# A two-layer hybrid trunk on one core: head 1's third attention group as a block product, transposes and scores behind other products

## The chip, the cores and the metric

The kernel runs on one core of a Trainium2 chip. The metric is the device time of one execution in microseconds (us), the median of several runs. A profiled execution is a run of its own with a hardware trace; its "span" is the part of it in which the trace sees instructions. Engines: PE (TensorE, the matrix unit; PEld is its weight load), DVE (VectorE), ACT (ScalarE), POOL (GpSimd) and SP (SyncE, which here only issues transfers). Each engine executes its own instructions strictly in the order in which the program holds them.

## The reference

The kernel computes two decoder layers for 512 tokens of width 1024 in float32. Layer 0 is the part that matters here, a dilated attention with 8 heads and 3 groups per head; layer 1 has a pooling mixer in its place, and a SwiGLU feed-forward network follows each.

```
qkv = (h @ w_qkv).reshape(B, S, 3, 3, HEADS, 128)        # 3 groups x (q, k, v) x 8 heads of 128
for g, (window, dil) in enumerate(((128, 1), (512, 4), (2048, 16))):
    o, lse = dilated_window_attention(q_g, k_g, v_g, window, dil, slopes[g])
...
wts = softmax(lse over the 3 groups)
o = sum over groups of wts * o
x = x + o.reshape(B, S, 1024) @ w_out
x = x + (silu(gate) * up) @ w_down                        # behind each mixer
```

So each head needs three q/k pairs (group 0, 1 and 2), the scores of group 0 and of groups 1 and 2, a softmax that is merged over the groups, and values for all three.

## The kernel before

**Products.** A float32 product is made of three matmuls on a high and a low part (hi x hi, hi x lo, lo x hi). The weights come from memory into a ring `raw` of 4 buffers, and ACT (L91, the high part) and DVE (L92, the low part) split them into a ring `w` of 5 buffers. A *plain* product (class `Product`, L325, L326, L328) turns 1024 inputs into 128 columns of q or k for 512 tokens: 24 matmuls of 128 x 512. A *block product* (`seven`, with `mult`, L457 to L459) makes q and k of a group together by Strassen's scheme, in seven products of 12 matmuls of 128 x 256 each; it costs 84 matmuls of half the width in place of 48 of the full one. For it DVE adds up inputs (tiles `T`, made by `prepare`, whose L574, L578, L579 and L583 are DVE work), DVE puts the results together (L498, L504 or L506, L511, L512; ACT copies the first, L485), and the weights need sums too (class `Pair`): SP issues the transfers `b` (L169), `a` (L170) and the half-size `c` (L171), POOL issues a transfer L172 that adds a further piece of memory into `b` once `b` has landed, and DVE adds L188 and L189. A pair is split in four steps, `blocks`, `sums`, `more`, `last`; the split of `sums` needs the accumulated `b`.

**Stages.** Head 0 and, up to `NSOLO`, the groups of head 1 use plain products; all other groups use `seven`. The values of group 0 of an even head and the odd head after it come from one more `seven` (results `vt`); the values of groups 1 and 2 come, after the odd head, from `values12` (L628 to L630; seven products of 24 matmuls of 128 x 256, with a pair of pairs as weights).

**What lies between the products.** After each of the seven products of `seven`, a *hook* (number 0 to 6) may emit other work of the attention. `between(h, g)` (L933) says what, for group `g` of head `h`:
- `scores0` (L712 on PE, 88 small matmuls; DVE L715, L718; ACT L721): scores of group 0.
- `scores12` (L732 and L736 on PE; DVE L739, L742; ACT L746): scores of groups 1 and 2; L732 needs q and k of group 1, L736 those of group 2.
- `scatter` (L753, DVE) and `merge` (L765 on PE; DVE L767 to L779; ACT L782): the merged softmax of a head.
- `turn0` (L795, 4 transposes on PE; ACT L799, L801; DVE L802) and `turn12` (L816, 4 transposes on PE; ACT L817; DVE L821): the probabilities are transposed.
- `turn_values` (L685, 8 transposes on PE; ACT copies): the values of group 0 are transposed, once for two heads.
- `output` (L833 to L843; 30 matmuls on PE): probabilities times values.

**What sets the order.** The program text sets it on PE. On the other engines a scheduler fixes it when the program is built; at run time each engine follows this list. Weights are requested (`pump`) between products, a load as soon as its `raw` buffers are free, a split as soon as its `w` buffer is.

Of the kernel before, what the change touches and what calls it, by code (L numbers as in the profile page):

```python
# [38 lines left out]
K2 = KC // 2  # L39
NPLAIN = 4  # L40
WARM = 5
NSOLO = 3
PARTS = ((0, 2, False), (2, 10, True), (10, 18, True), (18, 22, False))
ENDS = 5
BACK = {"blocks": 3, "sums": 7}
# [19 lines left out]
def trunk(ctx: ExitStack, tc: tile.TileContext, xT, xN, norms, w_first, w_qk, w_qkp, w_v0, w_v0p, w_v12, w_out, w_pair, w_down, w_dblock, w_pin, w_pgrp,  # L65
# [7 lines left out]
    def x_tile(k, name="x", dtype=F32):  # L73
        return cpool.tile([P, S], dtype, tag=f"x{k}", name=name)
# [7 lines left out]
    def ps():  # L82
        return psum.tile([P, S], F32, tag="ps", name="ps")
# [119 lines left out]
    def pump(n=1, must=False):  # L203

        turn[0] += not must
        for i in range(n):
            while loads and all(free(r, c) for r, c in loads[0][1].items()):
                loads[0][0].issued = turn[0]
                loads.popleft()[2]()
            if not steps or not free(steps[0][1]):  # L210
                assert not must
                return
            unit, back = steps[0][0], BACK.get(steps[0][2].__name__)
            if not must and back and unit.back and turn[0] < unit.issued + back:
                return
            steps.popleft()[2]()

    def pairs(*srcs, shift=LINE // 4, back=False):

        these = [Pair(src, shift, back) for src in srcs]  # L220
        for parts in zip(*(p.steps() for p in these)):
            steps.extend(parts)
        units.append((these,))
# [11 lines left out]
    def plain(*srcs, lean=False):  # L235
        for src in srcs:
            share(1, src, lean=lean)

    for h in range(HEADS):
        if h == 0:  # L240
            plain(*[w_qk[u] for u in range(len(QK) - NF)])
        for g in range(3):
            if h == 1 and g < NSOLO:
                plain(*[w_qk[len(QK) - NF + 2 * g + c] for c in range(2)])
            elif h:
                pairs(w_qkp[3 * h - 3 - NSOLO + g])
        if h == 0:
# [123 lines left out]
    def product(layer):  # L371
        return Product(KC, stream(layer)).add(range(KC)).p
# [77 lines left out]
    def in_place(t, a=slice(0, 2)):  # L450
        return t[:, a.start * H2:a.stop * H2]

    def mult(dst, w, half, T, name, n=K2, on=False):
        for k in range(n):
            c = slice(half * w.n + k * P, half * w.n + (k + 1) * P)
            th, tl = T[name, k]
            nc.tensor.matmul(dst, w.t[0][:, c], th, start=k == 0 and not on, stop=False, skip_group_check=on)  # L457
            nc.tensor.matmul(dst, w.t[0][:, c], tl, start=False, stop=False, skip_group_check=on)  # L458
            nc.tensor.matmul(dst, w.t[1][:, c], th, start=False, stop=k == n - 1, skip_group_check=on)  # L459

    def part(unit, name):
        while name not in unit.w:
            pump(must=True)
        return unit.w[name]

    def seven(T, one, two, scratch, after={}, blocks=False):


        (unit,), = units.popleft()
        into, left, right = by_block if blocks else in_place, slice(0, 1), slice(1, 2)  # L470

        def again(v):
            return v.unsqueeze(1).to_broadcast([P, 2, H2])

        p1, p26, p45, p73 = ps(), ps(), ps(), ps()

        def behind(i):
            pump()
            for f in after.get(i, ()):
                f()  # L480

        w = part(unit, "b")
        mult(p1[:, :H2], w, 0, T, "11")
        first, sums = scratch("first"), scratch("sums")
        nc.scalar.copy(first[:, :H2], p1[:, :H2])  # L485
        behind(0)
        mult(p26[:, :H2], w, 1, T, "21")
        w.done()
        behind(1)
        w = part(unit, "s")  # L490
        mult(p45[:, H2:], w, 0, T, "1")
        behind(2)
        mult(p73[:, :H2], w, 1, T, "3")
        w.done()
        behind(3)
        w = part(unit, "m")
        mult(p26[:, H2:], w, 0, T, "2")
        nc.vector.tensor_add(into(one), p26, again(first[:, :H2]))  # L498
        behind(4)
        mult(p73[:, H2:], w, 1, T, "22")  # L500
        w.done()
        if blocks:
            for a in (left, right):
                nc.vector.tensor_add(in_place(sums, a), in_place(p73, a), into(one, right))  # L504
        else:
            nc.vector.tensor_add(sums, p73, again(one[:, H2:]))  # L506
        behind(5)
        w = part(unit, "l")
        mult(p45[:, :H2], w, 0, T, "4")
        w.done()  # L510
        nc.vector.tensor_sub(into(two), p45, again(sums[:, :H2]))  # L511
        nc.vector.tensor_sub(into(one, right), sums[:, H2:], p45[:, H2:])  # L512
        behind(6)
# [82 lines left out]
    with tc.tile_pool(name="opool", bufs=1) as opool:  # L596
        early = opool.tile([P, HEADS, S], F32R, tag="o", name="early")
        with tc.tile_pool(name="apool", bufs=1) as apool:
# [9 lines left out]
            def evac(h, u, p):  # L608
                g, c = QK[u]
                t = apool.tile([P, S], F32, name=f"qk{g}{c}")  # L610
                scaled_by(t, p, g == 0)
                QKV[h, g, c] = t
# [64 lines left out]
            VT = []  # L677
# [174 lines left out]
            H, T, o = {}, {}, []  # L852
# [34 lines left out]
            def scratch(name):  # L887
                return apool.tile([P, S], F32, tag="scratch", name=name, bufs=3)
# [41 lines left out]
            def later(f, *a):  # L930
                return lambda: f(*a)

            def between(h, g):  # L933

                if g == 0:
                    if h % 2:
                        return {1: [later(merge, h - 1)]} if h == 1 else {}
                    return {1: [later(output, h - 2)], 2: [later(merge, h - 1)]}
                if g == (2 if h == 1 else 1):
                    turns = [later(turn0, h - 1), later(turn12, h - 1)]  # L940
                    if h % 2 and h > 1:
                        turns.append(later(turn_values, h - 1))
                    return {1: turns, 3: [later(scores0, h)]}
                return {}

            prepare(0)
            for u in range(NF):
# [17 lines left out]
            for h in range(1, HEADS):  # L965
                for g in range(3):
                    if h == 1 and g < NSOLO:
                        for c in range(2):
                            evac(h, 2 * g + c, product(0))
                        for fs in between(h, g).values():  # L970
                            for f in fs:
                                f()
                    else:
                        for c in range(2):
                            QKV[h, g, c] = apool.tile([P, S], F32, name=f"qk{g}{c}")
                        seven(T, QKV[h, g, 0], QKV[h, g, 1], scratch, between(h, g), g == 0)
                if h == 1:
                    whole = opool.tile([P, HEADS, S], F32, tag="o", name="o")
                    o.extend(whole[:, h, :] for h in range(HEADS))
                if h == HEADS - 1:  # L980
                    X[:] = [x_tile(k) for k in range(KC)]
                    for k in range(KC):
                        nc.gpsimd.dma_start(X[k], xN[:, k, :])
                if h % 2 == 0:
                    VT[:] = [apool.tile([P, S], F32, tag=tag, name="vt") for tag in ("row", "o0")]
                    seven(T, *VT, scratch, {0: [later(scores12, h)], 4: [later(scatter, h), later(output, h - 1)],
                                            5: [later(merge, h)]}, True)
                elif h < HEADS - 1:
                    QKV[h // 2, 12, 2] = values12({0: [later(scores12, h)], 4: [later(scatter, h)]})
                else:  # L990
                    QKV[h // 2, 12, 2] = values12({0: [later(scores12, h)], 1: [later(halve, 0), later(halve, 1)],
                                                   2: [later(scatter, h), later(halve, 2), later(halve, 3)],
                                                   3: [later(merge, h)],
                                                   4: [later(give, ("t", k, 0)) for k in range(2)]
                                                   + [later(halve, 4), later(halve, 5)]})
# [480 lines left out]
```

## Time and profile before

| | before |
|---|---|
| median of 3 runs | 1190.72 us (1189.71 to 1190.86) |
| the profiled execution | 1190.77 us |
| its span | 1187.8 us |
| granted TensorE clock, mean | 0.998 |
| attention of heads 1 to 7 in the span | from about 60 to 415 us |

The span is 3.0 us shorter than the profiled execution's own time. A row of the timeline view reads: start in us, duration in us, engine, line of the program, operation, output and input, shape, how many; in square brackets the idle time before it and the instruction that ended it. Matmuls are pipelined, so their durations overlap: the time that one costs is the distance between two starts. A row of the windows view reads: the stretch, its length, PE's busy time and the number of matmuls that touch the stretch, the granted clock, DMA's share and GB/s.

### The profile page before, as it was taken

The page shows a single profiled execution, that of the slowest core. Times are in us where ns is not written, and L with a number is a line of the kernel's source. Part 1 is how long each engine was busy: PE and PEld are TensorE (multiplying, and loading weights), DVE is VectorE, ACT ScalarE, POOL GpSimd, SP SyncE. Part 2 cuts the span into 40 slices and gives each one's busy share as a digit, 9 for nine tenths or more (in the row PEclk, how much of TensorE's full clock was granted, in tenths as well). Part 3 has the DMA queues.
Part 4 walks back from the last instruction along what each step waited for, and adds up shares of the span by engine and source line. Part 5 has one row for each costly group of instructions (what it writes and reads, how often), then busy time and mean ns, then how long its engine had stood idle before and what let it go on. Part 6 is the DMA issues. An engine that isn't in the chain of part 4 may idle for free.

```text
span 1187.8 us, 24866 instructions
## 1 busy us (share of the span) xinstructions
PE 1180.1 (99%) x9934; PEld 1119.3 (94%) x9934; DVE 965.5 (81%) x1693; ACT 711.1 (60%) x1243; POOL 168.8 (14%) x170
## 2 busy tenths in 40 slices
PE   9999999999999999999999999999999999999997
PEld 7889999999999988889999999988888999999997
DVE  7978988889797855699988997656879998898875
ACT  6545555455455546647756775675575775676553
POOL 1111211111111002311111111122130111111100
PEclk9999999999999999999999999999999999999999
DMA  8346666665766449857777777798695777777732
GB/s 293 116 104 163 156 155 158 169 162 147 193 158 155 143 142 212 184 118 188 198 193 191 195 184 199 202 265 210 125 198 107 191 193 198 200 193 191 198 93 71
DMA packets 82003, 205.18 MB, mean 173 GB/s; under 512 B 7760, under 2 KB 13024, under 8 KB 81888
## 3 DMA queue, kind: packets, MB, share of 16 engines
q1 hardware_dynamic: 51088, 141.96, 36.5%
q0 software_dynamic: 30512, 61.36, 31.2%
q8 instruction: 77, 1.26, 0.4%
q14 instruction: 38, 0.31, 0.1%
q10 hardware_dynamic: 288, 0.29, 0.1%
HBM read 201.48 MB, written 2.10 MB: 171 GB/s over the span
## 4 chain that ended last, share of the span: by engine, by line
PE 98%; issue 1%; ACT 0%; DVE 0%; POOL 0%; DVEq 0%; POOLq 0%
PE ps L457 20%; PE ps L459 19%; PE ps L458 19%; PE ps L325 9%; PE ps L328 8%; PE ps L326 8%; PE ps L628 2%; PE ps L629 2%; PE ps L630 2%; PE ps L918 2%; PE ps L840 1%; PE ps L712 1%; PE ps L732 1%; PE ps L834 1%; PE ps L833 0%
## 5 line engine op out<-in xcount | busy, mean ns | idle before, releaser
L91 ACT ACTIVATE w<-raw 128x1024 fp32r<-128x1024 f32 x265 | 280.6, 1063 | 175.5 <-PE ps L459 76.3
L92 DVE TENSOR_TENSOR w<-raw,w 128x1024 fp32r<-128x1024 f32 x265 | 322.8, 1221 | 58.6 <-ACT w L91 54.8
L457 PE MATMUL ps<-far,w 128*128 128x256 f32 x896 | 246.6, 275 | 0.3 <-ACT first L531 0.3
L458 PE MATMUL ps<-far,w 128*128 128x256 f32 x896 | 246.5, 275 | 0.0
L459 PE MATMUL ps<-far,w 128*128 128x256 f32 x896 | 246.4, 275 | 0.0
L457 PE MATMUL ps<-near,w 128*128 128x256 f32 x640 | 179.3, 280 | 0.0
L458 PE MATMUL ps<-near,w 128*128 128x256 f32 x640 | 177.1, 277 | 0.0
L459 PE MATMUL ps<-near,w 128*128 128x256 f32 x640 | 177.1, 277 | 0.0
L457 PEld LDWEIGHTS ps<-far,w 128*128 128x128 f32 x896 | 168.2, 188 | 0.5 <-ACT first L531 0.5
L458 PEld LDWEIGHTS ps<-far,w 128*128 128x128 f32 x896 | 168.2, 188 | 0.1
L459 PEld LDWEIGHTS ps<-far,w 128*128 128x128 f32 x896 | 168.2, 188 | 0.0
L325 PE MATMUL ps<-near,w 128*128 128x512 f32 (+1 forms) x332 | 125.6, 379 | 0.0
L328 PE MATMUL ps<-near,w 128*128 128x512 f32 (+1 forms) x332 | 124.9, 376 | 0.0
L326 PE MATMUL ps<-near,w 128*128 128x512 f32 (+1 forms) x332 | 124.9, 376 | 0.0
L457 PEld LDWEIGHTS ps<-near,w 128*128 128x128 f32 x640 | 120.5, 188 | 0.4
L458 PEld LDWEIGHTS ps<-near,w 128*128 128x128 f32 x640 | 120.3, 188 | 0.0
L459 PEld LDWEIGHTS ps<-near,w 128*128 128x128 f32 x640 | 120.3, 188 | 0.0
L172 POOL DMA_DIRECT2D raw<-w_pair x36 | 43.6, 1210 | 293.3 <-DMA raw<-w_pair 112.2
L325 PEld LDWEIGHTS ps<-near,w 128*128 128x128 f32 x332 | 62.3, 188 | 11.6 <-ACT near L91 0.4
L326 PEld LDWEIGHTS ps<-near,w 128*128 128x128 f32 x332 | 62.4, 188 | 11.3 <-DVE near L92 0.2
L328 PEld LDWEIGHTS ps<-near,w 128*128 128x128 f32 x332 | 62.3, 188 | 11.4
L91 ACT ACTIVATE half<-rawhalf 128x512 fp32r<-128x512 f32 x81 | 51.0, 630 | 14.7 <-PE ps L459 12.6
(310 smaller groups left out, 2758.2 us busy)
## 6 DMA issues: line engine op xcount, KB each, us to landing
raw<-w_pair SPq DMA_DIRECT2D x80, 512.0 KB, 5.0
raw<-w_qkp SPq DMA_DIRECT2D x36, 512.0 KB, 4.2
raw<-w_pair POOLq DMA_DIRECT2D x36, 512.0 KB, 7.4
raw<-w_dblock SPq DMA_DIRECT2D x32, 512.0 KB, 4.6
raw<-w_v SPq DMA_DIRECT2D x18, 512.0 KB, 4.6
raw<-w_qkp POOLq DMA_DIRECT2D x18, 512.0 KB, 7.6
rawhalf<-w_pair SPq DMA_DIRECT2D x36, 256.0 KB, 5.2
raw<-w_dblock POOLq DMA_DIRECT2D x16, 512.0 KB, 7.4
```

Source lines behind the costliest of these rows:

```text
L91: nc.scalar.activation(hi, v, AF.Copy)
L92: nc.vector.tensor_tensor(lo, v, hi.bitcast(F32), op=OP.subtract)
L172: nc.gpsimd.dma_start(self.b.rearrange("p (a c) -> p a c", a=2), self.src[:, None, 3 * n:].to_broadcast([P, 2, n]), accum_op=OP.add)
L325: nc.tensor.matmul(self.p[:, cols], w[0][:, s], mh[:, cols], start=self.done == 0, stop=False)
L326: nc.tensor.matmul(self.p[:, cols], w[0][:, s], ml[:, cols], start=False, stop=False)
L328: nc.tensor.matmul(self.p[:, cols], w[1][:, s], mh[:, cols], start=False, stop=self.done == self.n)
L457: nc.tensor.matmul(dst, w.t[0][:, c], th, start=k == 0 and not on, stop=False, skip_group_check=on)
L458: nc.tensor.matmul(dst, w.t[0][:, c], tl, start=False, stop=False, skip_group_check=on)
L459: nc.tensor.matmul(dst, w.t[1][:, c], th, start=False, stop=k == n - 1, skip_group_check=on)
L628: nc.tensor.matmul(o, mh, wh, start=k == 0, stop=False)
L629: nc.tensor.matmul(o, mh, wl, start=False, stop=False)
L630: nc.tensor.matmul(o, ml, wh, start=False, stop=k == K2 - 1)
```

## The change

`NSOLO` goes from 3 to 2, so that head 1's group 2 runs through `seven` (with a pair as weights) in place of two plain products. And `between` and the values' hooks place the attention's other work anew:

```diff
-NSOLO = 3
+NSOLO = 2
...
                 if g == 0:
-                    if h % 2:
-                        return {1: [later(merge, h - 1)]} if h == 1 else {}
-                    return {1: [later(output, h - 2)], 2: [later(merge, h - 1)]}
-                if g == (2 if h == 1 else 1):
-                    turns = [later(turn0, h - 1), later(turn12, h - 1)]
-                    if h % 2 and h > 1:
-                        turns.append(later(turn_values, h - 1))
-                    return {1: turns, 3: [later(scores0, h)]}
-                return {}
+                    return {1: [later(merge, h - 1)], 3: [later(turn_values, h - 1)] if h > 1 else []} if h % 2 else {
+                        1: [later(output, h - 2)], 2: [later(merge, h - 1)]}
+                if h == 1 and g:
+                    return {3: [later(turn0, 0)], 5: [later(turn12, 0)], 6: [later(scores0, 1)]} if g == 2 else {}
+                if g == 1:
+                    return {0: [later(turn0, h - 1)], 2 + h % 2: [later(turn12, h - 1)], 4: [later(scores0, h)]}
+                return {} if h % 2 else {2: [later(output, h - 1)]}
...
                 if h % 2 == 0:
                     VT[:] = [apool.tile([P, S], F32, tag=tag, name="vt") for tag in ("row", "o0")]
-                    seven(T, *VT, scratch, {0: [later(scores12, h)], 4: [later(scatter, h), later(output, h - 1)],
-                                            5: [later(merge, h)]}, True)
+                    seven(T, *VT, scratch, {3: [later(scores12, h)], 6: [later(scatter, h)]}, True)
```

So in head 1 `turn0` stands behind the fourth product of group 2, `turn12` behind the sixth and `scores0` behind the seventh. In heads 2 to 7 `turn0`, `turn12` and, in odd heads, `turn_values` no longer stand together but at three places; `scores0` stands one product later; the merge of an even head moves from the values' product into group 0 of the next head; `output` of an odd head moves from the values' product to group 2; and `scores12` of heads 2, 4 and 6 goes from the values' first product to the fourth. Lines behind L933 shift by two or three.

The change moves instructions also on the engines that the text does not order. First DVE's list while head 1's group 0 is computed, at the third input sum of `prepare` (L578 and what follows). Before:

```order
L743 TENSOR_SCALAR nm<-st 128x4
L606 TENSOR_TENSOR qk_698<-ps,row 128x16x16x2
L753 TENSOR_TENSOR far<-st,place 128x64
L92 TENSOR_TENSOR w<-raw,w 128x1024
L578 TENSOR_TENSOR raw<-raw 128x2x256
L579 TENSOR_TENSOR raw<-raw 128x256
L583 TENSOR_TENSOR raw<-raw 128x256
L574 SCALAR_TENSOR_TENSOR raw<-x,nrm,row 128x512
```

and now:

```order
L92 TENSOR_TENSOR near<-raw,near 128x512 x2
L606 TENSOR_TENSOR qk_729<-ps,row 128x16x16x2
L767 TENSOR_TENSOR far<-ps,place 128x64
L770 TENSOR_REDUCE st<-far 128x16
L92 TENSOR_TENSOR w<-raw,w 128x1024
L771 TENSOR_TENSOR mx<-st 128x8
L578 TENSOR_TENSOR raw<-raw 128x2x256
L772 TENSOR_TENSOR ex<-st,mx 128x16
L579 TENSOR_TENSOR raw<-raw 128x256
L774 TENSOR_TENSOR dd<-ex,st 128x16
L583 TENSOR_TENSOR raw<-raw 128x256
L775 TENSOR_TENSOR mx<-dd 128x8
```

Ahead of the first L578 there now stand the second result of group 0 (`qk_729`, the k product), the start of head 0's merge and one split `w` more, the one that needs the `w` buffer which that k product gives back.

Then DVE's list at the end of head 1's group 2 (`s_493`, `s_617` before and `s_496`, `s_620` now are head 0's probabilities; `qk_841`, `qk_873` before and `qk_821`, `qk_822` now are q and k of head 1's group 2). Before:

```order
L92 TENSOR_TENSOR w<-raw,w 128x1024 x2
L188 TENSOR_TENSOR raw<-raw 128x512
L189 TENSOR_TENSOR raw<-raw 128x512
L606 TENSOR_TENSOR qk_841<-ps,row 128x512
L92 TENSOR_TENSOR w<-raw,w 128x1024
L812 MEMSET t_893 128x512
L606 TENSOR_TENSOR qk_873<-ps,row 128x512
L791 MEMSET t_875 128x896
L92 TENSOR_TENSOR w<-raw,w 128x1024
L802 STREAM_TRANSPOSE t_875<-s_493 32x4x32 x4
L821 STREAM_TRANSPOSE t_893<-s_617 32x4x32 x4
```

and now:

```order
L188 TENSOR_TENSOR raw<-raw 128x512
L802 STREAM_TRANSPOSE t_884<-s_496 32x4x32 x4
L92 TENSOR_TENSOR w<-raw,w 128x1024 x3
L498 TENSOR_TENSOR qk_821<-ps,first 128x512
L189 TENSOR_TENSOR raw<-raw 128x512
L506 TENSOR_TENSOR sums<-ps,qk_821 128x512
L812 MEMSET t_933 128x512
L188 TENSOR_TENSOR raw<-raw 128x512
L92 TENSOR_TENSOR w<-raw,w 128x1024
L821 STREAM_TRANSPOSE t_933<-s_620 32x4x32 x4
L511 TENSOR_TENSOR qk_822<-ps,sums 128x512
L512 TENSOR_TENSOR qk_821<-sums,ps 128x256
```

Before, q and k of group 2 are finished by one L606 each. Now they are finished by L511 and L512, which stand last in this list, behind three splits in a row (L92 x3; the third of them is the `sums` step of the second pair of `values12`), a fourth split and the eight small transposes.

Last, DVE's list at the end of head 2's values (`vt`), from the second score of groups 1 and 2 (L739) on. Before:

```order
L739 SCALAR_TENSOR_TENSOR s_1747<-ps,b_1505 128x4x128
L739 SCALAR_TENSOR_TENSOR s_1747<-ps,b_1505 128x4x32
L92 TENSOR_TENSOR half<-rawhalf,half 128x512
L742 TENSOR_REDUCE st<-s_1747 128x4
L743 TENSOR_SCALAR nm<-st 128x4
L92 TENSOR_TENSOR w<-raw,w 128x1024
L753 TENSOR_TENSOR far<-st,place 128x64
L92 TENSOR_TENSOR w<-raw,w 128x1024
L498 TENSOR_TENSOR vt<-ps,first 128x16x16x2
```

and now:

```order
L742 TENSOR_REDUCE st<-s_1874 128x4
L504 TENSOR_TENSOR sums<-ps,vt 128x256
L743 TENSOR_SCALAR nm<-st 128x4
L504 TENSOR_TENSOR sums<-ps,vt 128x256
L188 TENSOR_TENSOR raw<-raw 128x512
L92 TENSOR_TENSOR w<-raw,w 128x1024
L511 TENSOR_TENSOR vt<-ps,sums 128x16x16x2
L512 TENSOR_TENSOR vt<-sums,ps 128x8x16x2
L753 TENSOR_TENSOR far<-st,place 128x64
L189 TENSOR_TENSOR raw<-raw 128x512
L767 TENSOR_TENSOR far<-ps,place 128x64
```

L753, which the matmul L765 of the merge needs, stood ahead of the values' sums; now it stands behind L511 and L512, which end the values.

## The prediction, made before the changed kernel was run

> **What bounds the kernel now.** I read the busy shares first, then the chain of waits, then PE's own waits.
>
> ```profile
> PE   1180.1 (99%) x9934; PEld 1119.3 (94%) x9934; DVE 965.5 (81%) x1693; ACT 711.1 (60%) x1243; POOL 168.8 (14%) x170
> PE 98%; issue 1%; ACT 0%; DVE 0%; POOL 0%; DVEq 0%; POOLq 0%
> PE ps L898 <- DVE idle L895: 1.2, 1, 1.2
> PE ps L457 <- ACT first L531: 0.3, 1, 0.3
> ```
>
> PE is busy for 99% of the span and the chain that ended last is PE for 98%. In the whole trace PE waits twice, 1.5 us together, neither time in the attention. So the time is PE's list. The change can save only what it takes off that list or off the pace at which it is worked through, and it can lose by any wait that it puts there. No wait exists that it could remove.
>
> **Pace.** One 128x256 matmul does not always cost the same. These windows lie between two interruptions each, in heads 1 to 3; the first is plain products, the others hold, by the code, 12, 24, 132, 48, 120, 24 and 120 block matmuls.
>
> ```profile
> 65.69:87.55 21.86, 21.86 (x99) 1.00 0.44 114
> 116.60:118.10 1.50, 1.50 (x15) 1.00 0.72 247
> 127.30:130.30 3.00, 3.00 (x27) 1.00 0.60 175
> 131.60:146.69 15.09, 15.09 (x141) 1.00 0.72 183
> 148.06:153.82 5.76, 5.76 (x58) 1.00 0.66 187
> 158.70:172.41 13.71, 13.71 (x124) 1.00 0.58 133
> 174.07:177.08 3.01, 3.01 (x28) 1.00 0.65 202
> 178.37:192.62 14.25, 14.25 (x129) 1.00 0.47 106
> ```
>
> ```profile
> 126.39 0.28 PE L459 MATMUL ps<-h,w 128*128 128x256 f32 x1
> 126.51 0.60 PE L795 MATMUL ps<-ident,s 128*128 128x128 f32 x4
> 126.94 0.60 PE L816 MATMUL ps<-ident,s 128*128 128x128 f32 x4
> 127.30 0.36 PE L457 MATMUL ps<-near,w 128*128 128x256 f32 x1
> 127.50 0.28 PE L458 MATMUL ps<-near,w 128*128 128x256 f32 x1
> 127.62 0.28 PE L459 MATMUL ps<-near,w 128*128 128x256 f32 x1
> 131.60 0.39 PE L457 MATMUL ps<-near,w 128*128 128x256 f32 x1
> 131.82 0.28 PE L458 MATMUL ps<-near,w 128*128 128x256 f32 x1
> ```
>
> Behind an interruption the first step takes 0.20 to 0.22 us (127.30 to 127.50, 131.60 to 131.82), some 0.09 more than the steps after it. Those then run at one of two paces until the next interruption: (15.09 - 0.22) / 131 = 113.5 ns in the window from 131.60 and (14.25 - 0.22) / 119 = 117.9 ns in the one from 178.37, at a granted clock of 1.00 in both. The price of the slow pace is 4.4 ns per matmul. By the same arithmetic the stretch from 148.06 (behind `scores12` in the values of an even head) is slow, (5.76 - 0.22) / 47 = 117.9, and the one from 158.70 (behind a merge) fast, (13.71 - 0.22) / 119 = 113.4; the short ones from 116.60 (behind `output` in group 0) and 127.30 and 174.07 (behind the transposes) are slow, with a second long step at their end. Behind `scores0` the even head is fast (131.60) and the odd one slow (178.37). Heads 4 to 7 repeat this.
>
> **The change, part by part.** First the product. The first window is groups 1 and 2 of head 1, four plain products, 96 matmuls: group 2 costs half, 10.93 us. In its place come 84 block matmuls, 9.5 us at the fast pace and 9.9 at the slow one. I take 9.7: **-1.2 us**. `turn0`, `turn12` and `scores0` of head 1 stood together and now interrupt three times: 2 x 0.09 = **+0.2**.
>
> Second, head 1's wait. PE's list around it was:
>
> ```profile
> 87.55 0.60 PE L795 MATMUL ps<-ident,s 128*128 128x128 f32 x4
> 89.81 0.39 PE L628 MATMUL ps<-w,near 128*128 128x256 f32 x1
> 92.67 1.05 PE L732 MATMUL ps<-qk,qk 128*128 128x128 f32 x8
> 93.66 0.46 PE L736 MATMUL ps<-qk,qk 128*32 128x32 f32 x32
> ```
>
> With group 2 1.0 us shorter, PE comes to L736 at 93.66 - 1.0 = 92.7. L736 needs L511 and L512, now last in DVE's list, behind three splits of which the third needs the accumulated `b` of the second values pair. How late that is follows from these rows of DVE, ACT, SP and POOL:
>
> ```profile
> 65.87 1.04 ACT L91 ACTIVATE w<-raw 128x1024 fp32r<-128x1024 f32 x1
> 62.90 0.69 DVE L578 TENSOR_TENSOR raw<-raw 128x512 f32<-128x512 f32 x1
> 69.22 1.22 DVE L92 TENSOR_TENSOR w<-raw,w 128x1024 fp32r<-128x1024 f32 x1
> 70.36 0.42 DVE L583 TENSOR_TENSOR raw<-raw 128x256 f32<-128x256 f32 x1
> 70.84 0.33 SPq L169 DMA_DIRECT2D raw<-w_v  x1
> 75.27 1.25 POOL L172 DMA_DIRECT2D raw<-w_v  x1 [0.27 <-ACT ex L773]
> raw<-w_v SPq DMA_DIRECT2D x1, 512.0 KB, 3.8
> raw<-w_v POOLq DMA_DIRECT2D x1, 512.0 KB, 6.6
> raw<-w_qkp POOLq DMA_DIRECT2D x1, 512.0 KB, 7.4
> DMA to landing us min/median/max: 6.5/7.6/10.6
> ```
>
> Now a split stands ahead of the first L578, and its `w` buffer comes free when PE ends group 0's k product, at the start of the first window, 65.69. ACT's half ends at about 66.9 (as the row at 65.87 does), DVE's 1.2 later, at 68.1. So L578 starts 5.3 us later than at 62.90. From L578 to the end of the second L583 it was 70.78 - 62.90 = 7.9, a split of 1.2 included that now stands elsewhere, and small steps of the merge come in, about half a microsecond: 7.2. The second L583 ends at 75.3, not 70.8; it frees the `raw` buffer that SP's load waits for (SP issued 0.06 after it). The load lands 3.8 later, at 79.1; POOL issues the accumulation at 79.7 (75.27 came 0.6 behind the landing at 70.84 + 3.8); it lands after 6.6 to 7.4, at 86.3 to 87.1. ACT's split takes 1.06 and DVE's 1.2 behind it: the third split ends at 88.6 to 89.4. Then come, by these rows,
>
> ```profile
> 144.34 0.68 DVE L188 TENSOR_TENSOR raw<-raw 128x512 f32<-128x512 f32 x1
> 143.74 0.68 DVE L498 TENSOR_TENSOR qk<-ps,first 128x512 f32<-128x512 f32 x1
> 146.67 0.68 DVE L511 TENSOR_TENSOR qk<-ps,sums 128x512 f32<-128x512 f32 x1
> 147.27 0.41 DVE L512 TENSOR_TENSOR qk<-sums,ps 128x256 f32<-128x256 f32 x1
> 87.20 0.48 DVE L812 MEMSET t<- 128x512 f32 x1 [2.12 <-PE ps L328]
> 91.65 1.25 DVE L821 STREAM_TRANSPOSE t<-s 32x128 f32<-32x128 f32 x4
> ```
>
> L498, L189, L506 and L188 at 0.6 from start to start, the memset 0.5, a split 1.15, the transposes 1.25, L511 0.6 and L512 0.35: 6.25. L512 ends at 94.9 to 95.7, and PE waits 2.2 to 3.0. I take **+2.5**. The bounds: the POOL row of all such transfers in the attention has 6.5 to 10.6 and a median of 7.6, so from 2.1 up to about 6; below, PE waits for nothing if the load is earlier than I count. Behind L736 on PE stands all of the rest; DVE's scores and ACT's exponentials behind it shift along and have the values' six products left. Their own reader, the merge in head 2, comes two stages later.
>
> The Trainium skill, "DMA: Bandwidth & Descriptors", section "Anatomy of one DMA — SWDGE (gpsimd) path", fits a transfer issued through GpSimd with 2.0 us plus its bytes over 436 GB/s. For 512 KB that is an estimate of 3.2 us; the landing would come at about 83 and the wait be gone, which is rival A's time. The trace disagrees (6.6 us for this one, 6.5 at least for any).
>
> Third, interruptions in heads 2 to 7. `turn0` and `turn12` part (6 times), `turn_values` leaves them (3 times); `output`, `merge` and both scores only move. Nine first steps of 0.09: **+0.8**.
>
> Fourth, pace. Per pair of heads I go through the hooks and give each stretch the pace that its kind of interruption has in the trace. Before, slow are 12, 24, 48, 24 and 120 of the windows, 228. Now, even head: 12 behind `output`; 24 behind `turn0` and 24 behind `turn12`; 36 behind `scores12`, going on for 24 in the odd head's group 0; there 48 behind `turn_values`, 36 behind `turn0`, 12 behind `turn12`, and 108 behind `scores0`: 324. Open are the 96 behind `output` in group 2, so 324 to 420, or 96 to 192 more. Three pairs at 4.4 ns give +1.3 to +2.5; I take **+1.9**. Since the rule that makes a stretch slow isn't in the trace, the bounds are wide: all stretches fast, -228 x 3 x 4.4 ns = -3.0; all 588 of a pair slow, +4.8.
>
> Sum: -1.2 + 0.2 + 2.5 + 0.8 + 1.9 = +4.2. The profiled execution took 1190.77 us, 0.05 above the median of the runs shown; with it the time is 1195.0. Everything else moved is hidden: DVE's and ACT's sums lie beside 99% busy PE, and no other buffer of head 1's group 2 is due earlier than the DVE list above gives it.
>
> **Rivals.** A: *head 1's wait doesn't come*, because the second pair's load starts as early as before (70.84) or its accumulation isn't last. For it: what holds the load is a chain of four engines that I count without a trace. Or the accumulation lands 2.5 sooner; against that, none of the attention's took under 6.5, and it took 6.6 here. Against the first: the rows name each step. Then 1195.0 - 2.5 = 1192.5.
>
> B: *the pace falls the other way* (not slower): if not the kind of interruption but its place among the seven products makes a stretch slow, then moving `scores12` (48 slow matmuls behind it, now 36) and the transposes may leave all of them fast, -3.0 in place of +1.9: 1190.1, and with A too, 1187.6. It decides where no more matmuls are slow than before: then the other terms' sum, +2.3, lies within the measurement's bound (below). For it: even and odd heads differ behind the same `scores0`. Against: all stretches behind transposes are slow.
>
> C: *the merges of even heads wait*, three times. L753 now stands behind L511 and L512 of the values, which need their last product; L511, L512 and L753 take 0.6 + 0.35 + 0.2 = 1.2 behind it, and L765 follows two products later, 24 x 0.1135 = 2.7 us. That leaves 1.5 us. A split ahead of them that comes late by its own length on ACT and DVE, 2.2 us, would turn this into 0.7, and one accumulation more (the 10.6 of the row above against its median of 7.6) into 1 or more: about 3 in all. Then 1198. Against: PE gives back the `w` buffers long before, by the trace's lack of any such wait.
>
> **How the numbers follow.** Less than 0.2%, 2.4 us, can't be told from no change here, so "faster" is below 1188.3 and "slower" above 1193.1. My forecast has 0.45 (own range 1193.0 to 1197.5), A 0.20, B 0.20, C 0.15. Slower: 0.43 of the forecast, 0.02 of A and all of C, 0.60. Faster: 0.08 of B and 0.03 of A, 0.11. The rest, 0.29, is the same. The range goes from 1189.5 (most of B) to 1199 (C, or a slow accumulation).
>
> **What would show it.** PE's waits should have one row more, L736 on DVE's L512, of 2 to 3 us, at 92 to 96 us; the third split of the DVE list should wait for ACT, and that for the accumulated transfer landing at 86 to 87. Without that row A holds. Windows between the interruptions of heads 2 and 3 should show 117.9 ns behind transposes and 113.5 behind merges; if those behind `turn0` are fast, B. A wait of L765 in heads 3, 5 and 7 would be C. I am wrong if PE's waits still sum to 1.5 us and the time is below 1190.

## The result, and the profile after

The changed kernel takes 1193.74 us (median of 18 runs, 1189.71 to 1195.16) against 1190.31 us before (18 runs, 1189.71 to 1191.29): ratio 1.0028, 95% interval 1.0022 to 1.0034, so 3.4 us slower. The runs of the change also spread over 5.4 us, where those of before spread over 1.6. The profiled execution took 1192.90 us, its span is 1191.0 (before 1187.8).

The page's busy shares, its chain by engine, and PE's waits, of the changed kernel:

```profile
PE 1179.6 (99%) x9970; PEld 1120.6 (94%) x9970; DVE 968.4 (81%) x1699; ACT 712.8 (60%) x1246; POOL 173.8 (15%) x171
PE 93%; DVE 3%; DMA 1%; issue 1%; ACT 1%; POOL 0%; DVEq 0%; POOLq 0%; ACTq 0%
PE ps L736 <- DVE qk L511: 3.7, 1, 3.7
PE ps L898 <- DVE idle L895: 1.2, 1, 1.2
PE ps L457 <- ACT first L531: 0.3, 1, 0.3
```

PE is busy 0.5 us less than before, and yet the span is 3.2 us longer: a wait of L736 on L511 has come in, and the chain now leaves PE for 7% of the span. This is that part of the chain, in order of time (start, duration, what; "issue" is time for which the profile shows no releaser):

```profile
48.34 7.05 DMA raw<-w_qkp
...
55.60 3.46 issue
59.06 0.69 DVE raw L188
...
63.94 1.24 DVE w L92
...
69.00 1.13 DVE w L92
70.13 0.17 DVE mx L771
70.30 0.60 DVE raw L578
...
81.48 6.52 DMA raw<-w_v
88.15 1.07 ACT w L91
89.24 1.23 DVE w L92
90.47 0.60 DVE qk L498
```

It begins with the accumulation for head 1's own group 2, a transfer that the kernel before does not have at this place. Its issue at 48.34 and DVE's L188 at 59.06 enclose it; L188 reads the sum, and everything behind L188 in DVE's list has to wait with it. The DMA issues in that stretch (out, in, queue, count, size, median us to landing) and DVE's row for L188 say how long:

```profile
raw<-w_v SPq DMA_DIRECT2D x2, 512.0 KB, 8.4
raw<-w_qkp POOLq DMA_DIRECT2D x1, 512.0 KB, 10.6
59.06 0.69 DVE L188 TENSOR_TENSOR raw<-raw 128x512 f32<-128x512 f32 x1 [3.47 <-issue]
```

The accumulation took 10.6 us, with two full loads for the values beside it. From there DVE stays one to two us behind the times of the prediction, down to the splits and to L511.

The wait costs more than its 3.7 us. These windows of PE around and behind it are 3.41 us long each (length, busy time and count, granted clock, DMA share, GB/s):

```profile
90.93:94.34 3.41, 1.76 (x16) 1.00 0.15 20
94.34:97.75 3.41, 1.33 (x38) 1.00 0.97 137
97.75:101.16 3.41, 3.41 (x19) 0.51 0.91 345
101.16:104.57 3.41, 3.41 (x31) 0.99 0.40 72
```

In the third window PE works without a pause at half its clock: 19 matmuls where the fourth has 31. One takes 0.21 us there and 0.114 elsewhere; 16 of them are 16 x 0.1 = 1.6 us. So the wait costs 4.0 (from L732 to the next matmul of the values 91.64 to 97.01, 5.37, in place of 92.67 to 94.05), and the half clock behind it 1.6 more.

Heads 2 to 7 went the other way. One window per pair of heads, before:

```profile
110.51:213.24 102.73, 102.73 (x1103) 1.00 0.66 162
213.24:315.95 102.71, 102.71 (x1103) 1.00 0.67 163
315.95:410.65 94.70, 94.70 (x1032) 1.00 0.62 154
```

and after (the same first and last instruction each):

```profile
115.12:217.48 102.36, 102.36 (x1103) 1.00 0.68 163
217.48:319.70 102.22, 102.22 (x1102) 1.00 0.68 163
319.70:413.90 94.20, 94.20 (x1032) 1.00 0.63 155
```

They are 0.37, 0.49 and 0.50 shorter, 1.4 us together. These parts add up to the difference of the spans: -1.1 (head 1's group 2 as a block product, to the start of its values), +4.0 (wait), +1.6 (half clock), -1.4 (heads 2 to 7), +0.1 (rest) = +3.2.

### The profile page after: what moved, and what is told of

Same layout as the page of the kernel before. It is cut to its first block, busy times and chain, and to the rows that moved or that the text cites. A ratio compares the mean times of both kernels' runs of the same rounds, so it can differ in the third digit from the quotient of the medians.

```text
span 1191.0 us, 24969 instructions
## 1 busy us (share of the span) xinstructions
PE 1179.6 (99%) x9970; PEld 1120.6 (94%) x9970; DVE 968.4 (81%) x1699; ACT 712.8 (60%) x1246; POOL 173.8 (15%) x171
## 4 chain that ended last, share of the span: by engine, by line
PE 93%; DVE 3%; DMA 1%; issue 1%; ACT 1%; POOL 0%; DVEq 0%; POOLq 0%; ACTq 0%
PE ps L457 20%; PE ps L459 19%; PE ps L458 19%; PE ps L325 7%; PE ps L326 7%; PE ps L328 7%; PE ps L628 2%; PE ps L629 2%; PE ps L630 2%; PE ps L918 2%; PE ps L840 1%; PE ps L712 1%; PE ps L834 1%; DMA raw<-w_qkp 1%; DVE w L92 1%
## 5 line engine op out<-in xcount | busy, mean ns | idle before, releaser
L92 DVE TENSOR_TENSOR w<-raw,w 128x1024 fp32r<-128x1024 f32 x266 | 324.1, 1222 | 49.2 <-ACT w L91 45.3
L457 PE MATMUL ps<-near,w 128*128 128x256 f32 x656 | 184.8, 282 | 0.0
L458 PE MATMUL ps<-near,w 128*128 128x256 f32 x656 | 181.4, 276 | 0.0
L459 PE MATMUL ps<-near,w 128*128 128x256 f32 x656 | 181.3, 276 | 0.0
L457 PEld LDWEIGHTS ps<-near,w 128*128 128x128 f32 x656 | 123.4, 188 | 0.4
L458 PEld LDWEIGHTS ps<-near,w 128*128 128x128 f32 x656 | 123.3, 188 | 0.0
L459 PEld LDWEIGHTS ps<-near,w 128*128 128x128 f32 x656 | 123.3, 188 | 0.0
L325 PEld LDWEIGHTS ps<-near,w 128*128 128x128 f32 x332 | 62.3, 188 | 11.6 <-ACT near L91 0.4
L328 PEld LDWEIGHTS ps<-near,w 128*128 128x128 f32 x332 | 62.3, 188 | 11.6
L326 PEld LDWEIGHTS ps<-near,w 128*128 128x128 f32 x332 | 62.4, 188 | 11.2 <-DVE near L92 0.2
L188 DVE TENSOR_TENSOR raw<-raw 128x512 f32<-128x512 f32 x82 | 56.0, 683 | 4.9 <-issue 3.5
```

The source lines that it names most:

```text
L92: nc.vector.tensor_tensor(lo, v, hi.bitcast(F32), op=OP.subtract)
L188: nc.vector.tensor_add(a[:, :n], a[:, :n], b[:, :n])
L325: nc.tensor.matmul(self.p[:, cols], w[0][:, s], mh[:, cols], start=self.done == 0, stop=False)
L326: nc.tensor.matmul(self.p[:, cols], w[0][:, s], ml[:, cols], start=False, stop=False)
L328: nc.tensor.matmul(self.p[:, cols], w[1][:, s], mh[:, cols], start=False, stop=self.done == self.n)
```

## The experiments

Each is an edit of the changed kernel unless another base is named. The times of before that stand beside them are 1190.0 to 1190.2 us.

**Which half of the change loses.** First head 1's part alone. The edit puts `between` for heads 2 to 7 and the values' hooks back:

```diff
...
-                    return {0: [later(turn0, h - 1)], 2 + h % 2: [later(turn12, h - 1)], 4: [later(scores0, h)]}
-                return {} if h % 2 else {2: [later(output, h - 1)]}
+                    turns = [later(turn0, h - 1), later(turn12, h - 1)]
+                    if h % 2 and h > 1:
+                        turns.append(later(turn_values, h - 1))
+                    return {1: turns, 3: [later(scores0, h)]}
+                return {}
...
-                    seven(T, *VT, scratch, {3: [later(scores12, h)], 6: [later(scatter, h)]}, True)
+                    seven(T, *VT, scratch, {0: [later(scores12, h)], 4: [later(scatter, h), later(output, h - 1)],
+                                            5: [later(merge, h)]}, True)
```

> Head 1 as in the change (block product, turn0, turn12 and scores0 behind the fourth, sixth and seventh product), heads 2 to 7 as before. Theory W (the loss is head 1's wait for q and k of group 2, 4.0 us in the changed kernel's profile, and 1.6 us of slow matmuls right behind it; head 1's shorter product gives 1.05 back): slower than before by 4.0 to 5.2 us, near 1194.9, with one wait of L736 on L511 of about 3.7 us. Rival P (the loss comes from the pace of the matmuls and the parted transposes in heads 2 to 7): no change or 1 us faster, near 1189.5.

Measured: 1194.89 us (5 runs), ratio 1.0046 (1.0032 to 1.0059). PE's waits in its profile:

```profile
PE ps L736 <- DVE qk L511: 3.9, 1, 3.9
PE ps L898 <- DVE idle L895: 1.2, 1, 1.2
PE ps L732 <- ACT t L799: 0.4, 1, 0.4
```

Then the other part alone: `NSOLO = 3`, head 0's transposes and head 1's `scores0` together again behind the plain products, the new hooks in heads 2 to 7.

```diff
-NSOLO = 2
+NSOLO = 3
...
-                    return {3: [later(turn0, 0)], 5: [later(turn12, 0)], 6: [later(scores0, 1)]} if g == 2 else {}
+                    return {1: [later(turn0, 0), later(turn12, 0)], 3: [later(scores0, 1)]} if g == 2 else {}
```

> Head 1 as before (plain products, transposes and scores0 together), heads 2 to 7 as in the change. Theory W: faster than before by 1.0 to 1.8 us, near 1188.9, since from the start of head 2 to the end of the attention the changed kernel's profile is 1.4 us shorter than before's; no wait of PE in the attention. Rival P: slower than before by 2 us or more.

Measured: 1188.70 us, ratio 0.9990 (0.9982 to 0.9999, barely clear of no change), no wait of PE in the attention. +4.85 and -1.3 make +3.5, against the +3.4 of the whole change; it is about the sum of its two parts, as theory W has it, and P is out.

**Is it the wait, and can it be stepped around?** Head 1's scores of groups 1 and 2 behind the second product of its values:

```diff
-QKV[h // 2, 12, 2] = values12({0: [later(scores12, h)], 4: [later(scatter, h)]})
+QKV[h // 2, 12, 2] = values12({1 * (h == 1): [later(scores12, h)], 4: [later(scatter, h)]})
```

> The change, but head 1's scores of groups 1 and 2 stand behind the second product of its values in place of the first, 24 matmuls or 2.75 us later. Theory W: DVE's list ahead of L511 stays, so the wait shrinks from 3.7 to 0.8 to 1.3 us. If the slow matmuls behind the wait come only after a long wait, the time is near 1189.3; if any wait brings them, near 1190.9. Rival P: no change from the changed kernel's 1193.7.

Measured: 1189.68 us (1187.18 to 1190.66), ratio 0.9995 (0.9986 to 1.0004); no wait of PE in the attention of the profiled run, which is the second fastest (1187.84) and in which the accumulation landed after 9.6 us, one microsecond less than in the change. Whether the slower runs wait was not traced. Behind the third product:

```diff
-QKV[h // 2, 12, 2] = values12({0: [later(scores12, h)], 4: [later(scatter, h)]})
+QKV[h // 2, 12, 2] = values12({2 * (h == 1): [later(scores12, h)], 5 if h == 1 else 4: [later(scatter, h)]})
```

> The change, but head 1's scores of groups 1 and 2 stand behind the third product of its values (5.5 us later than in the change) and its scatter one product later. Theory W: no wait at L736 and no slow matmuls, 1193.7 - 5.6 = 1188.1, faster than before by about 2.2 us. Rival D (DVE is late there altogether, and something behind the scores waits in place of L736): a new wait of 1 us or more in head 1 or 2 and 1189.5 or more. Rival P: 1193.7.

Measured: 1189.99 us (1187.97 to 1191.87), ratio 1.0002 (0.9993 to 1.0011). Rival D holds here in part. L736 no longer waits, but the accumulation took 13.0 us in the profiled run (1191.87, the slowest), and then the values themselves wait:

```profile
PE ps L628 <- ACT t L799: 2.0, 1, 2.0
PE ps L898 <- DVE idle L895: 1.2, 1, 1.2
PE ps L629 <- DVE w L92: 0.9, 1, 0.9
```

L628 here opens the values' second product, whose weights the first has used already; by the profile it waits for a result buffer `ps`, which ACT gives back with its copies of `turn0` (L799), and these ran behind a split whose transfer landed at 91.2. L629 then waits for a split. So moving the reader takes away the loss of that place, and the lateness of DVE and ACT finds the next reader. How much of it varies from run to run two profiles of two kernels can't say.

**What makes it late.** The two loads beside the accumulation go through POOL's queue, behind it:

```diff
-            nc.sync.dma_start(self.b, self.src[:, :2 * n])
-            nc.sync.dma_start(self.a, self.src[:, n:3 * n])
+            eng = getattr(self, "eng", nc.sync)
+            eng.dma_start(self.b, self.src[:, :2 * n])
+            eng.dma_start(self.a, self.src[:, n:3 * n])
...
+            if h == 1:
+                units[-1][0][0].eng = nc.gpsimd
```

> The change, but the two full-size loads of the first values pair of head 1 (a and b, 512 KB each) go through POOL's queue behind the accumulation for head 1's group 2, and no longer through SP's beside it. Theory C (what makes head 1 late is this accumulation: it took 10.6 us in the changed kernel's profile, since the two loads run beside it, and DVE idles 3.5 us at L188 for it): it lands after 6.5 to 7.5 us, DVE's idle time at L188 shrinks below 0.7 us, the wait of L736 to 1.2 to 2.2 us, no slow matmuls follow, and the time is 1189 to 1190.5. Rival Q (it is long by itself, whatever runs beside it): still 9 us or more, wait and time as in the changed kernel, 1193.7.

Measured: 1191.26 us (1188.84 to 1191.85), ratio 1.0002 (0.9993 to 1.0011), outside the expected range. The accumulation took 8.2 us, not 6.5 to 7.5, and not the 9 of rival Q: between the two. DVE's idle time at L188 fell to 1.07, the wait of L736 (L739 in this kernel's lines) to 1.8 us, which theory C expected. The half clock came all the same, against the expectation:

```profile
89.04:92.45 3.41, 3.41 (x69) 1.00 0.08 18
92.45:95.86 3.41, 1.62 (x43) 1.00 0.86 119
95.86:99.27 3.41, 3.41 (x25) 0.53 0.92 339
```

With hook 1 added:

> The same, with head 1's scores of groups 1 and 2 also behind the second product of its values. Theory C: no wait of PE in head 1 in any run, so all runs are near the shortest of the run with hook 1 alone, 1187.2 to 1187.8, with a spread below 1 us: faster than before by about 2.7 us. Rival Q: no better than hook 1 alone, 1189.7 with a spread of 3 us.

Measured: **1187.17 us** (1186.85 to 1187.49), ratio 0.9972 (0.9960 to 0.9983), 6 runs. PE waits in the two places outside the attention where it always did, and nowhere else; the spread is 0.6 us. This is faster than both kernels, by 3.1 and 6.6 us.

Two more runs hold the loads back until the next product instead, so that nothing of the values runs beside the accumulation:

```diff
-            while loads and all(free(r, c) for r, c in loads[0][1].items()):
+            while loads and all(free(r, c) for r, c in loads[0][1].items()) and turn[0] >= getattr(loads[0][0], "hold", 0):
...
+            if h == 1:
+                units[-1][0][0].hold = 5
```

> The change, but the loads of the first values pair are held back until one product later, by when the input sums of prepare have taken the raw buffers; so nothing runs beside the accumulation for head 1's group 2, and the scheduler puts L188 further back in DVE's list. Theory C (the accumulation is long because of the loads beside it): it lands 6.4 to 7.5 us after its issue at 48, and DVE doesn't idle for it. The wait of L736 is then at most 1 us, unless the values' pairs, which come later now, take its place: their second accumulation would land after 90 us and the values' third product wait 1 us or more for it. 1188 to 1190 in the first case, 1191 and more in the second. Rival Q (long by itself): 9 us or more again.

Measured: 1192.74 us (1191.00 to 1193.45), ratio 1.0020 (1.0010 to 1.0029). The accumulation still took 8.1 us, so C is right only in part: with both loads beside it on SP it took 9.2 to 13.0 in six profiles, without them 8.1, and another in the kernel before 6.6. What makes up the rest was not found; the pair's own second load (L170, 48.14 to 52.18 in this profile) still runs beside it. L736 waits no more, but the time is lost at neither of the two places that were expected (the lines of this kernel are two higher):

```profile
PE ps L687 <- DVE vt L608: 2.0, 1, 2.0
PE ps L767 <- DVE far L755: 1.6, 1, 1.6
```

With the raw buffers free for it earlier, the scheduler puts the first part of `prepare` ahead of the second of group 0's value tiles (L608) in DVE's list, and the transposes of the values (L687) and the merge (L767) of head 0 wait for DVE. And the first of the two waits has half a clock behind it, 11 matmuls of 128 x 512 in a stretch that holds 17 of them at full clock:

```profile
53.02:56.43 3.41, 1.41 (x40) 1.00 0.50 93
56.43:59.84 3.41, 3.41 (x11) 0.50 0.00 0
```

With the change's own account, -1.1 + 2.0 + 1.6 + 1.6 - 1.4 = +2.7 is an estimate of the loss; measured is +2.6.

> The same, with head 1's scores of groups 1 and 2 behind the second product of its values: no wait of L736 in either case. If nothing takes its place, 1187.2 as with POOL's loads and hook 1; if the values' pairs come too late, 1 to 3 us more.

Measured: 1192.69 us, ratio 1.0020 (1.0011 to 1.0029), the same two waits and the same half clock. It is 5.5 us above 1187.2, more than the 1 to 3 that were expected. This way was a dead end.

**One link of DVE's list, and the clock.** `turn12` of head 0 one product later:

```diff
-return {3: [later(turn0, 0)], 5: [later(turn12, 0)], 6: [later(scores0, 1)]} if g == 2 else {}
+return {3: [later(turn0, 0)], 6: [later(turn12, 0), later(scores0, 1)]} if g == 2 else {}
```

> The change, but turn12 of head 0 stands behind the seventh product with scores0 in place of the sixth: DVE's list has its transposes (1.25 us) and L188 (0.55 us) behind L511 and L512 in place of ahead. Theory W: the wait shrinks from 3.7 to about 1.9 us. The matmuls behind it keep their pace if a wait of about 2 us is too short for the halved clock, then 1193.7 - 1.8 - 1.6 = 1190.3; if not, 1191.9. Rival (the wait hangs on the accumulated transfer alone and not on DVE's list): 3.7 us and 1193.7.

Measured: 1191.62 us (1189.19 to 1193.20), ratio 1.0010 (1.0001 to 1.0019), a wait of 2.2 us with an accumulation of 10.8 us, landing 6.6 us ahead of head 0's merge as in the change. So `turn12`'s transposes and one L188 ahead of L511 in DVE's list make up 1.5 of the 3.7, by one profile each; the expectation had 1.8. And again half a clock behind it:

```profile
88.42:91.83 3.41, 3.41 (x83) 1.00 0.50 159
91.83:95.24 3.41, 1.25 (x11) 1.00 0.35 39
95.24:98.65 3.41, 3.38 (x44) 0.50 0.98 220
```

A wait of 2.3 us in the run that comes next (`scores0` at hook 3) did not bring it. It falls into two windows, of which PE is busy for more than half each:

```profile
90.50:93.92 3.42, 2.16 (x20) 1.00 0.56 56
93.92:97.33 3.41, 2.38 (x47) 1.00 1.02 289
```

Where such windows begin is worked out at the end.

**What made heads 2 to 7 faster.** That run is the change with `turn12` at hook 2 and `scores0` at hook 3 in heads 2 to 7:

```diff
-return {0: [later(turn0, h - 1)], 2 + h % 2: [later(turn12, h - 1)], 4: [later(scores0, h)]}
+return {0: [later(turn0, h - 1)], 2: [later(turn12, h - 1)], 3: [later(scores0, h)]}
```

> The change, but in heads 2 to 7 turn12 stands behind the third product in odd heads too and scores0 behind the fourth, where it stood before. If the place of scores0 decides on the pace behind it, the 120 matmuls behind it in odd heads are slow again, 14.25 us for 120. If what stands ahead of it decides (the transposes now parted), they stay fast, 13.7 us. One look, so the time says little.

Measured, in a single run of 1190.24 us: the 120 matmuls behind `scores0` in head 3 take 13.73 us, fast, at the place where they took 14.25 before. So the place does not decide. What stands ahead can be tried on the kernel before, with `turn_values` of odd heads alone moved to hook 3 of group 0:

```diff
-                        return {1: [later(merge, h - 1)]} if h == 1 else {}
+                        return {1: [later(merge, h - 1)]} if h == 1 else {3: [later(turn_values, h - 1)]}
...
-                    if h % 2 and h > 1:
-                        turns.append(later(turn_values, h - 1))
```

> The kernel before with one part of the change alone: in heads 3, 5 and 7 turn_values stands behind the fourth product of group 0 and no longer with turn0 and turn12 in group 1. If the three transposes standing together are what made the 120 matmuls behind scores0 of odd heads slow (14.25 us against 13.73 in the run with scores0 back at its old place), these are fast now: 0.5 us less per odd head, less 0.1 for the added interruption, 1.2 us in all, near 1189.0. Rival: they stay at 14.25 us and the time goes up by 0.3 us, since the slow pace hangs on something else that stands there.

Measured: 1189.49 us, ratio 0.9996 (0.9987 to 1.0005). Windows of head 5, the 60 matmuls behind `turn_values` and the 120 behind `scores0`:

```profile
268.97:276.13 7.16, 7.16 (x64) 1.00 0.72 148
281.21:294.94 13.73, 13.73 (x129) 1.00 0.59 134
```

The 120 are fast now, as expected. But the 60 behind the moved transposes, fast before as part of a stretch of 120 behind the merge, became slow, (7.16 - 0.21) / 59 = 117.8 ns, so less than half of the expected 1.2 us is left, and that isn't clear of no change. Nor do the transposes that stand together make the 120 slow by themselves. The run with head 1's part alone has the code of before in heads 2 to 7, and there the 120 are fast in heads 3 and 5 and slow only in head 7 (heads 3 and 7):

```profile
184.27:198.00 13.73, 13.73 (x130) 1.00 0.45 98
388.94:403.19 14.25, 14.25 (x130) 1.00 0.48 116
```

So the pace of a stretch hangs on what ran ahead of it, further back than the last interruption, and these runs give no rule for it.

Last, the second scores of even heads, put back from hook 3 to hook 0 in the fastest kernel:

```diff
-                    seven(T, *VT, scratch, {3: [later(scores12, h)], 6: [later(scatter, h)]}, True)
+                    seven(T, *VT, scratch, {0: [later(scores12, h)], 6: [later(scatter, h)]}, True)
```

> The run with POOL's loads and hook 1 (1187.17 us), with one part of the change undone: scores12 of heads 2, 4 and 6 behind the first product of the values again, in place of the fourth. Theory: it was no gain, since L736 did not wait there before (no wait of PE in the attention): within 0.5 us of 1187.2, with waits of L736 in heads 2, 4 and 6 of at most 0.3 us each. Rival: with the values' transposes and output moved, DVE is later there, and each of the three waits 1 us or more: 1190 or above.

Measured: 1187.70 us, ratio 0.9983 (0.9974 to 0.9992), no wait of L736 there, as in the kernel before. It is 0.5 us more than 1187.17. The pace is a part of that, since 96 matmuls behind `scores12` are slow now, in place of 60, and each pair of heads is 0.16 us longer in the profile, 0.5 in all. Another 0.3 is lost at the kernel's start, ahead of anything that this edit touches, where PE waits once for ACT (L921, 0.5 us); so the two medians don't tell the one from the other:

```profile
252.94:264.36 11.42, 11.42 (x107) 1.00 0.70 167
```

## Why the prediction was right, and where only by luck

The time (1195.0 forecast, 1193.7 measured), the direction and the place of the loss were right. Of the four terms one was right, and the errors of the others partly cancel: head 1's wait was forecast 3.1 us too small, heads 2 to 7 were forecast 4.1 us too large. That the time came within 1.3 us is in good part luck.

- *The product, -1.0 with its interruptions*: -1.1. Right.
- *Head 1's wait, +2.5*: +5.6, of which 4.0 is the wait and 1.6 the half clock. The mechanism was the forecast one, down to the waiting instruction, L736 behind DVE's L511 and L512, and the third split waiting for the values' second accumulation. The step that failed is "DVE's 1.2 later, at 68.1. So L578 starts 5.3 us later": (68.1 - 62.90 is 5.2; nothing rests on the difference.) L578 started at 70.2, because DVE was not free. It had idled for 3.5 us at L188, which stands ahead in its list, for the accumulation of head 1's own pair. The sum took the spread of such transfers (6.5 to 10.6) for the accumulation of the values' second pair alone, which then took 6.5; the one of head 1's own pair took 10.6. Four profiles with the same list of DVE from L188 to L512 and the reader at hook 0 agree: the later this accumulation lands, measured from head 0's merge (L765), the longer the wait.

| run | landing before L765 | wait of L736 |
|---|---|---|
| loads on POOL's queue | 9.0 us | 1.8 us |
| scores0 at hook 3 | 8.2 us | 2.3 us |
| the change | 6.6 us | 3.7 us |
| head 1's part alone | 5.9 us | 3.9 us, and 0.4 at L732 |

  In the profiles the landing varies by microseconds, so it may well be why the times of the change spread; a landing early enough would explain its run of 1189.71, but that run has no trace. The clock has its part too: the mean granted clock is 0.995 in five of the six slowest runs (1194.25 to 1195.16) and 0.997 to 0.999 in all others, which points to more than one stretch at half clock in them.
- The half clock behind the wait, 1.6 us, was in no term and no bound.
- *Interruptions, +0.8*: the first steps came as forecast (about 0.1 each), but transposes that stand alone are cheaper than together: four of L795 take 0.354 from the first start to the next instruction in place of 0.437, and L816 gains the same where L685 followed it. The term is about +0.2.
- *Pace, +1.9*: about -1.5. The step that failed is to "give each stretch the pace that its kind of interruption has in the trace". These are stretches of heads 4 and 5 after the change, behind `turn0` (24 matmuls), `turn12` (24), `output` (96), `scores12` (60), `turn_values` (48) and `scores0` of the odd head (108):

```profile
232.47:235.30 2.83, 2.83 (x28) 1.00 0.02 6
235.65:238.66 3.01, 3.01 (x28) 1.00 0.80 223
250.15:261.13 10.98, 10.98 (x99) 1.00 0.63 146
262.50:269.68 7.18, 7.18 (x71) 1.00 0.70 148
273.44:278.99 5.55, 5.55 (x51) 1.00 0.83 169
286.73:299.10 12.37, 12.37 (x118) 1.00 0.54 126
```

  With 0.21 for the first step, the second and the fourth are slow (the second with a long last step), the others fast, at 113.4 to 113.9 ns. The forecast had 324 of a pair slow; 228 of these (behind `turn0`, `turn_values`, and the odd head's `turn12` and `scores0`) run fast, and so do the 96 that it left open. 12 + 24 + 60 = 96 slow ones are left, where before it was 228: rival B's direction, and half of its size.
- *Rivals.* A did not hold in the profile of the change; its one run of 1189.71 has none. C did not occur: no wait of L765. B's mechanism was there and given 0.20, as an alternative to the forecast; it came together with it.

## What to carry to other kernels

Where the main engine is 99% busy, price a moved step by the lists of the engines beside it: which instruction in a strict list first waits for a transfer, and what stands behind it. Give a new transfer the widest duration that the trace shows for its kind, not the median, where loads run beside it, and then ask who reads its result first. Here a wait of 1.8 us on the matrix unit cost 1.6 more by the clock behind it, and one of 2.3 us did not, by where it fell.

## What the runs showed of the hardware

**Half a clock after a short wait.** The granted clock fell to 0.50 for one stretch of 3.41 us after waits of 3.7, 3.9, 2.2 and 1.8 us in head 1's values and after one of 2.0 in head 0 (loads held back), and not after 2.3 and 2.0 (scores behind the third product). The length of the wait doesn't sort these. What does can be read from the record of the granted clock in the 14 traces. Every change of the clock lies a whole number of times 3.413 us behind the first change of its trace; in the change these are 27, 28 and 346 times. The first one comes 4.4 to 7.3 us after the span's start, a little different each time. So the clock is set in windows of 3.41 us that run on whatever PE does, and a wait falls into them by chance. This is how long PE is busy in those windows around a wait, and the clock of the window that follows each:

| profile, wait | busy us of 3.41 | clock of the next window |
|---|---|---|
| the change, 3.7 | 1.72, then 1.38 | 1.00, then 0.50 |
| head 1's part alone, 3.9 | 1.79, then 0.73 | 1.00, then 0.50 |
| loads on POOL's queue, 1.8 | 1.62 | 0.50 |
| `turn12` later, 2.2 | 1.26 | 0.50 |
| `scores0` at hook 3, 2.3 | 2.16, then 2.38 | 1.00, then 1.00 |
| scores behind the third product, 2.0 | 1.93, then 2.87 | 1.00, then 1.00 |
| loads held back, 2.0 at L687 | 1.41 | 0.50 |
| the same with hook 1, 2.0 at L687 | 1.42 | 0.50 |

Up to 1.62 us the next window has half the clock, from 1.72 us on it has the full one. So the limit lies near half of a window. It can't be told more sharply: at the end of the program, where no matmul follows, 1.89 us brought the half clock in the kernel before and 1.99 did not in the one with `turn_values` apart, and the ends of matmuls are modelled. Whether a wait of some 2 us costs 1.6 us more is therefore chance, unless the wait is moved or cut. The two runs with the loads held back fit: 4 of their 22 times lie at 1191.0 and the others at 1192.3 to 1193.5, some 1.6 above, though only two of the others have a trace. The Trainium skill, "TensorE: Matmul & The Clock Gate", section "What's actually happening", has such a window of 3413 ns, free-running; these traces agree with both. The same page's section "Why this matters for your kernels" asks only that idle gaps stay below about 3 us; here 1.8 us was enough.

**Two paces of one matmul.** At a granted clock of 1.00, 128x256 matmuls keep 113.5 or 117.9 ns until the next interruption. In all profiles in which L736 does not wait in head 1, heads 2 and 3, 4 and 5, and 6 and 7 show the same paces at the same places, so it is no noise, and a microsecond or two of 1190 are to be had by the order alone. In the five profiles in which L736 waits there, heads 2 and 3 differ from heads 6 and 7, with head 1's part alone also heads 4 and 5, though the code is the same. So the pace also depends on what happened many microseconds before. What sets it stays open.

**An accumulating transfer beside loads.** 512 KB that POOL's queue adds to a tile took 6.5 us for the two values pairs of head 1 in the change, and for head 1's own pair 9.2 to 13.0 with two further loads beside it on SP, 8.0 to 8.3 where these were held back or put behind it in POOL's queue. In the change those loads took 8.4 us, before 5.5.
